# A macaron block with an RWKV mixer: where the second feed-forward layer's modulation chunks are begun

## The chip, the cores and the metric

The kernel runs on one NeuronCore of a Trainium2 chip. The metric is device time in microseconds. A run's time is that of one execution; the kernel before was run three times and profiled once more. Engines are named as the profile names them: PE is TensorE (PEld its weight loads), DVE is VectorE, ACT is ScalarE, POOL is GpSimd and SP is SyncE, which here only issues transfers.

## The reference

One block of 256 tokens with 2048 features. Three sublayers follow one another (a feed-forward layer, a mixer, a second feed-forward layer), each with its own shift, scale and gate out of one modulation vector:

```
mod = (silu(c) @ w_ada + b_ada).reshape(B, 3, 3, D_MODEL)      # w_ada is 2048 x 18432
def swiglu(h, w_gate, w_up, w_down):                            # D_FF = 5632
    return (silu(h @ w_gate) * (h @ w_up)) @ w_down
def sandwich_sublayer(x, fn, gain_pre, gain_post, shift, scale, gate, weight):
    h = rms_norm(x, gain_pre) * (1 + scale) + shift
    y = rms_norm(fn(h), gain_post)
    return x + weight * (1 + gate) * y
x = sandwich_sublayer(x, ffn1,  ..., mod[0, 0], mod[0, 1], mod[0, 2], 0.5)
x = sandwich_sublayer(x, mixer, ..., mod[1, 0], mod[1, 1], mod[1, 2], 1.0)
x = sandwich_sublayer(x, ffn2,  ..., mod[2, 0], mod[2, 1], mod[2, 2], 0.5)
```

All of it is float32. The kernel keeps that precision by splitting each operand into a rounded high part and the remainder (hi and lo) and adding three matmuls.

## The kernel before, in words

**A weight's way.** `load` (L167) has SP issue one transfer into one of four raw buffers. `split` (L173) casts it to hi on ACT (L179), then takes the difference lo on DVE (L180); hi and lo have four buffers each. `mm3` (L186) issues three matmuls per 128 x 128 piece (L189 hi x hT hi, L190 hi x hT lo, L191 lo x hT hi). hT holds the layer's input, transposed, in sixteen feature tiles of 128, each as hi and lo.

**The head of a feed-forward layer.** `outer` (L569) walks over five blocks of features, `FIRST_BLOCKS`: 2, 2, 4, 4 and 4 feature tiles, which the text calls blocks 1 to 5. `q` counts them from 0, and `i` counts ten weight loads in each: two for the first four tiles of the hidden layer (i = 0, 1), eight more (i = 2 to 9) for sixteen further tiles, whose sums are added up in SBUF (L604 a copy on ACT, L606 an addition on DVE). In block 1 those eight are left out and only their `tick` is called; block 2 then loads them for the feature tiles of blocks 1 and 2 at once (the merged loads, 1 MB each). So block 1 has 48 matmuls, block 2 has 48 + 8 x 48, and blocks 3 to 5 have 480 each.

Each block begins with `block(...)`: it finishes the modulation chunk that its features need, updates and scales the residual rows (L517 on DVE, L338 on ACT), transposes them on PE (L353), and makes hT with scale and shift (L357 and L361 on ACT, L362 the difference on DVE).

**A modulation chunk.** The shift and scale (vectors 7 and 6) of one block of features are one chunk, so chunk 3 is that of block 3. `ada_step` (L220) does a quarter of a chunk. For chunks 3, 4 and 5 a step is four tiles of 128 x 1024 in four buffers of their own, each by two transfers of 256 KB on SP (L238), and for each tile one product on DVE: `acc = tile * csilu[k] + acc` (L242 for a chunk's first, L244 for the others). After the fourth step, eight matmuls with a single column (L251, written x8 in the order and x16 in the trace) add up `acc` over partitions, and DVE adds the bias (L264). There is one `acc` buffer. PE, DVE, ACT and SP each work through their own list in order.

**What sets the order.** A scheduler writes the list of each engine before the run, from the program's order and priorities. A step stands in the program where `tick` (called after each load, and for each load left out) or `ada_finish` calls it. In the second layer a step is called at i in `TICKS = (1, 3, 7)` of every block as long as chunk 5 is not done. Chunks 1 and 2 are made in the mixer stage (`ADA_AHEAD = 1`). Three chunks or twelve steps are left: three in each of the blocks 1 to 4. Chunk 3's fourth step so falls into block 2, and chunk 4 ends and chunk 5 begins in block 3.

Of the kernel before, what the change touches and what calls it, by code (L numbers as in the profile page):

```python
# [25 lines left out]
MERGE = 4  # L26
FIRST_BLOCKS = ((0, 2), (2, 2), (4, 4), (8, 4), (12, 4))
TICKS = (1, 3, 7)
GROUPS = (20, 16, 8)
ADA_AHEAD = 1  # L30
ADA_FFN1, ADA_MIXER, ADA_OUT, ADA_FFN2 = 2.8, 3, 3, 12
# [45 lines left out]
class Block:  # L77
# [1124 lines left out]
    def run(self):  # L1202
        I = self.I
        self.constants()
        with ExitStack() as ph:
            mm, actp = self.ffn_pools(ph)
            self.begin(mm)

            def block(k0, n):
                q = [b[0] for b in FIRST_BLOCKS].index(k0)  # L1210
                self.ada_finish(((1, 0), q), mm)
                for tt in range(2):
                    self.pre_rows(tt, k0, n)
                self.pre_block(0, k0, n, mm)

            def tick(q, i):
                if q == len(FIRST_BLOCKS) - 1:
                    if i == 0:
                        self.begin_rest(mm)
                elif i in TICKS:  # L1220
                    self.ada_step(mm)

            self.ffn(I["ffn1_w_gate"], I["ffn1_w_up"], I["ffn1_w_down"], ADA_FFN1, mm, actp, FIRST_BLOCKS, block, tick,
                     FF_OUTER, FF_SPILL, (FF_SPILL + FF_OUTER) // 2 - 8, GROUPS,
                     lambda *a: (self.ada_finish((3,), mm), self.post_begin(0, 0.5, True, mm, *a)), lambda tt: None, True)
        with ExitStack() as ph:
            self.phase(ph, 2, 0, 2, 300)
            self.mixer(ph)
        with ExitStack() as ph:
            mm, actp = self.ffn_pools(ph)  # L1230

            def block(k0, n):
                self.ada_finish(((7, 6), [b[0] for b in FIRST_BLOCKS].index(k0)), mm)
                self.next_block(2, k0, n, mm)

            def tick(q, i):
                if i in TICKS and self.ada_pos < self.ada_end[(7, 6)]:
                    self.ada_step(mm)

            self.ffn(I["ffn2_w_gate"], I["ffn2_w_up"], I["ffn2_w_down"], ADA_FFN2, mm, actp, FIRST_BLOCKS,  # L1240
                     block, tick, FF_OUTER, FF_SPILL, (FF_SPILL + FF_OUTER) // 2 - 8, GROUPS,
                     lambda *a: (self.ada_finish((8,), mm), self.post_begin(2, 0.5, False, mm, *a)),
                     self.store, False)
# [27 lines left out]
```

## Time and profile before

| | before |
|---|---|
| median of three runs | 2172.55 us (2161.99 to 2174.09) |
| the profiled execution's own time | 2168.19 us |
| span of that execution | 2166.3 us |
| mean granted clock of TensorE | 0.986 |
| PE, DVE, ACT busy | 96%, 76%, 50% of the span |
| read from HBM | 497.77 MB |

The span runs from the first to the last instruction; the profiled execution's own time has another 1.9 us around it. The second layer's blocks 1 to 5 lie at 1378 to 1650 us of the span. In a timeline a row has its start, its length (us), engine, line, operation, output and input, count, and in brackets the idle time of that engine before it with what ended it. A row of the windows gives for each engine its busy time and, after an x, its instructions, then the granted clock, the DMA share and GB/s.

### The profile page before, as it was taken

To read this page: it belongs to the slowest core of one execution; us is meant where nothing else is said; L and a number is where in the kernel's file an instruction comes from. 1 tells how busy PE (TensorE), PEld (TensorE's weight loads), DVE (VectorE), ACT (ScalarE), POOL (GpSimd) and SP (SyncE) were. 2 spreads that over 40 slices of the span, in tenths; PEclk is the share of its full clock that TensorE was granted. 3 is DMA by queue.
4 is the path that set the end of the run, shared out by engine and by line. 5 is a ranking of instruction groups with operands and counts; after the bars stand their busy time and mean duration, and the time that the engine had idled before them with its cause. 6 is when DMAs were issued, how large, how long until landed. Compare 5 with 4: busy or idle time off the path is not lost.

```text
span 2166.3 us, 38214 instructions
## 1 busy us (share of the span) xinstructions
PE 2076.9 (96%) x15435; PEld 1828.5 (84%) x15435; DVE 1635.6 (76%) x2543; ACT 1078.5 (50%) x1809; POOL 0.2 (0%) x4
## 2 busy tenths in 40 slices
PE   4999999999999998999999999789999999999998
PEld 3999988888888877888888868689998888888886
DVE  6789897888878778887778776868899655555556
ACT  4534543444433555765656655444454344443453
POOL 0000000000000000000000000000000000000000
PEclk9999999999999999999999999889999999999999
DMA  9999888998888748625332335698888656555553
GB/s 314 359 319 321 282 291 303 330 319 310 310 318 297 270 137 247 195 83 164 103 105 84 99 98 175 233 346 282 305 284 297 237 193 195 186 183 194 195 187 125
DMA packets 313408, 502.40 MB, mean 232 GB/s; under 512 B 12965, under 2 KB 173838, under 8 KB 312974
## 3 DMA queue, kind: packets, MB, share of 16 engines
q1 hardware_dynamic: 311212, 496.32, 68.1%
q10 hardware_dynamic: 2018, 3.62, 0.5%
q8 instruction: 121, 1.98, 0.4%
q14 instruction: 57, 0.47, 0.1%
HBM read 497.77 MB, written 2.12 MB: 231 GB/s over the span
## 4 chain that ended last, share of the span: by engine, by line
PE 79%; DMA 9%; DVE 7%; ACT 3%; issue 2%; SPq 1%; DVEq 0%; ACTq 0%
PE mm L196 15%; PE mm L191 9%; PE mm L190 9%; PE mm L189 9%; PE mm L197 8%; DMA ada<-in_w_ada_dram 6%; PE mm L523 6%; PE mm L524 6%; PE mm L525 6%; DVE lo L180 3%; DVE acc L244 2%; DMA raw<-in_w_in_dram 1%; ACT hi L179 1%; DMA raw<-in_ffn_w_gate_dram 1%; PE mm L251 1%
## 5 line engine op out<-in xcount | busy, mean ns | idle before, releaser
L179 ACT CAST hi<-raw 128x1024 fp32r<-128x1024 f32 (+2 forms) x766 | 694.3, 913 | 798.1 <-PE mm L525 262.8
L180 DVE TENSOR_TENSOR lo<-raw,hi 128x1024 fp32r<-128x1024 f32 (+2 forms) x766 | 797.8, 1051 | 339.7 <-ACT hi L179 336.0
L196 PE MATMUL mm<-hT,hi 128*128 128x512 f32 x1536 | 539.8, 395 | 0.0
L190 PE MATMUL mm<-hT,hi 128*128 128x256 f32 x1824 | 521.6, 287 | 5.4 <-DVE hT L362 5.4
L189 PE MATMUL mm<-hT,hi 128*128 128x256 f32 x1824 | 518.5, 287 | 7.2 <-ACT hT L357 5.6
L191 PE MATMUL mm<-hT,lo 128*128 128x256 f32 x1824 | 522.7, 288 | 1.3 <-DVE lo L180 1.3
L197 PE MATMUL mm<-hT,lo 128*128 128x256 f32 x1536 | 431.8, 281 | 1.6 <-DVE lo L180 1.6
L244 DVE SCALAR_TENSOR_TENSOR acc<-ada,csilu,acc 128x1024 f32<-128x1024 f32 (+1 forms) x300 | 352.5, 1175 | 90.2 <-DMA ada<-in_w_ada_dram 85.7
L189 PEld LDWEIGHTS mm<-hT,hi 128*128 128x128 f32 x1824 | 347.1, 192 | 13.8 <-ACT hT L357 8.3
L190 PEld LDWEIGHTS mm<-hT,hi 128*128 128x128 f32 x1824 | 348.5, 191 | 10.8 <-DVE hT L362 7.5
L191 PEld LDWEIGHTS mm<-hT,lo 128*128 128x128 f32 x1824 | 347.5, 191 | 7.2 <-DVE lo L180 1.9
L196 PEld LDWEIGHTS mm<-hT,hi 128*128 128x128 f32 x1536 | 288.8, 188 | 67.7
L197 PEld LDWEIGHTS mm<-hT,lo 128*128 128x128 f32 x1536 | 288.0, 187 | 2.4 <-DVE lo L180 2.2
L524 PE MATMUL mm<-lo,act 128*128 128x512 f32 (+1 forms) x656 | 252.2, 384 | 0.4 <-DVE lo L180 0.4
L523 PE MATMUL mm<-hi,act 128*128 128x512 f32 (+1 forms) x656 | 252.4, 385 | 0.0
L525 PE MATMUL mm<-hi,act 128*128 128x512 f32 (+1 forms) x656 | 251.9, 384 | 0.0
L524 PEld LDWEIGHTS mm<-lo,act 128*128 128x128 f32 x656 | 123.3, 188 | 25.6 <-DVE lo L180 1.5
L523 PEld LDWEIGHTS mm<-hi,act 128*128 128x128 f32 x656 | 123.3, 188 | 24.5
L525 PEld LDWEIGHTS mm<-hi,act 128*128 128x128 f32 x656 | 123.3, 188 | 24.4
L606 DVE TENSOR_TENSOR act<-act,mm 128x512 f32<-128x512 f32 x96 | 64.2, 682 | 1.9 <-PE mm L191 1.6
L251 PE MATMUL mm<-ones,acc 128*128 128x1 f32 x128 | 18.6, 273 | 34.5 <-DVE acc L244 34.5
L251 PEld LDWEIGHTS mm<-ones,acc 128*128 128x128 f32 x128 | 18.3, 226 | 35.3 <-DVE acc L244 35.2
(371 smaller groups left out, 1965.6 us busy)
## 6 DMA issues: line engine op xcount, KB each, us to landing
raw<-in_ffn_w_down_dram SPq DMA_DIRECT2D x88, 1024.0 KB, 6.2
raw<-in_ffn_w_gate_dram SPq DMA_DIRECT2D x86, 1024.0 KB, 6.9
raw<-in_ffn_w_up_dram SPq DMA_DIRECT2D x86, 1024.0 KB, 5.5
ada<-in_w_ada_dram SPq DMA_DIRECT2D x160, 512.0 KB, 7.0
ada<-in_w_ada_dram SPq DMA_DIRECT2D x256, 256.0 KB, 5.3
raw<-in_w_in_dram SPq DMA_DIRECT2D x34, 1024.0 KB, 6.1
raw<-in_w_out_dram SPq DMA_DIRECT2D x16, 1024.0 KB, 5.3
raw<-in_w_in_dram SPq DMA_DIRECT2D x9, 512.0 KB, 4.6
```

The source lines that it names most:

```text
L179: a = nc.scalar.copy(hi, raw)
L180: d = nc.vector.tensor_tensor(lo, raw, hi.bitcast(F32), ALU.subtract)
L189: nc.tensor.matmul(ps, hi, x[:, 0, :], start=start, stop=False)
L190: nc.tensor.matmul(ps, hi, x[:, 1, :], start=False, stop=False)
L191: nc.tensor.matmul(ps, lo, x[:, 0, :], start=False, stop=stop)
L196: nc.tensor.matmul(ps.rearrange("p a t -> p (a t)"), hi, x.rearrange("p a t -> p (a t)"), start=start, stop=False)
L197: nc.tensor.matmul(ps[:, 0, :], lo, x[:, 0, :], start=False, stop=stop)
L244: self.later(nc.vector.scalar_tensor_tensor(acc, raw[:, i], ck, acc, ALU.mult, ALU.add))
L523: nc.tensor.matmul(ps, x[:, 0, ts], hi, start=start, stop=False)
L524: nc.tensor.matmul(ps, x[:, 0, ts], lo, start=False, stop=False)
L525: nc.tensor.matmul(ps, x[:, 1, ts], hi, start=False, stop=stop)
L606: nc.vector.tensor_tensor(part, part, bank, ALU.add)
```

## The change

In the second feed-forward layer the steps are called at other places: none in block 1, after loads 3, 5, 7 and 9 in block 2, and after loads 1, 3, 5 and 7 in blocks 3 and 4. Each of the chunks 3, 4 and 5 is so begun and ended within one block, the one before the block that needs it. The number of steps, tiles and matmuls is the same.

```
@@ -26,6 +26,7 @@
 FIRST_BLOCKS = ((0, 2), (2, 2), (4, 4), (8, 4), (12, 4))
 TICKS = (1, 3, 7)
+TICKS2 = ((3, 5, 7, 9), (1, 3, 5, 7))
@@ -1234,7 +1235,7 @@
             def tick(q, i):
-                if i in TICKS and self.ada_pos < self.ada_end[(7, 6)]:
+                if q and i in TICKS2[q > 1] and self.ada_pos < self.ada_end[(7, 6)]:
                     self.ada_step(mm)
```

One line is added near the top, so each line number of the changed kernel is one higher than before (L251 becomes L252). The rows below are the lists of three engines.

SP's list at the head of the second layer, before; `raw` are weight tiles (128x2x512 of blocks 1 and 2, 128x4x512 merged), `ada` modulation tiles:

```order
L169 DMA raw_15827<-in_ffn_w_gate_dram 128x2x512
L169 DMA raw_15861<-in_ffn_w_up_dram 128x2x512
L238 DMA ada_15864<-in_w_ada_dram 128x512 x2
L238 DMA ada_15868<-in_w_ada_dram 128x512 x2
L238 DMA ada_15872<-in_w_ada_dram 128x512 x2
L238 DMA ada_15876<-in_w_ada_dram 128x512 x2
L169 DMA raw_15962<-in_ffn_w_gate_dram 128x2x512
L238 DMA ada_15912<-in_w_ada_dram 128x512 x2
L238 DMA ada_15916<-in_w_ada_dram 128x512 x2
L238 DMA ada_15920<-in_w_ada_dram 128x512 x2
L238 DMA ada_15924<-in_w_ada_dram 128x512 x2
L169 DMA raw_15992<-in_ffn_w_up_dram 128x2x512
```

And the same place now:

```order
L170 DMA raw_15827<-in_ffn_w_gate_dram 128x2x512
L170 DMA raw_15861<-in_ffn_w_up_dram 128x2x512
L170 DMA raw_15913<-in_ffn_w_gate_dram 128x2x512
L170 DMA raw_15943<-in_ffn_w_up_dram 128x2x512
L239 DMA ada_16038<-in_w_ada_dram 128x512 x2
L239 DMA ada_16042<-in_w_ada_dram 128x512
L170 DMA raw_15973<-in_ffn_w_gate_dram 128x4x512
L170 DMA raw_16035<-in_ffn_w_up_dram 128x4x512
L239 DMA ada_16042<-in_w_ada_dram 128x512
```

The four weight tiles of blocks 1 and 2 now stand together, and three modulation transfers stand ahead of the first merged load, where 26 stood before. After that SP's list alternates two merged loads with the eight transfers of a step.

PE's list around the reduction of chunk 3, before; `mm` are the banks of sums, `acc` the chunk's products:

```order
L190 MATMUL mm_15804<-hT_94,hi_16021 128x256
L191 MATMUL mm_15804<-hT_94,lo_16022 128x256
L251 MATMUL mm_16010<-ones_71,acc_15863 128x1 x8
L189 MATMUL mm_16051<-hT_94,hi_16053 128x256
L190 MATMUL mm_16051<-hT_94,hi_16053 128x256
```

And now:

```order
L191 MATMUL mm_16397<-hT_94,hi_16426 128x256
L192 MATMUL mm_16397<-hT_94,lo_16427 128x256
L252 MATMUL mm_16474<-ones_71,acc_16037 128x1 x8
L190 MATMUL mm_16485<-hT_94,hi_16487 128x256
L191 MATMUL mm_16485<-hT_94,hi_16487 128x256
```

It stood behind the two small loads of block 2 (row 7721 of the list), ahead of all merged ones; it now stands behind seven of the eight merged loads (row 8057), 48 matmuls before block 3's transposes. In block 3 the reduction of chunk 4 has moved from behind three of the ten loads (row 8252) to behind seven (row 8444), and that of chunk 5 has kept its place in block 4 (row 8927).

DVE's list in block 3 at chunk 4's last products, before; `lo` are splits:

```order
L244 SCALAR_TENSOR_TENSOR acc_16113<-ada_16811,csilu_95,acc_16113 128x1024
L180 TENSOR_TENSOR lo_16772<-raw_16739,hi_16771 128x1024
L244 SCALAR_TENSOR_TENSOR acc_16113<-ada_16815,csilu_95,acc_16113 128x1024
L180 TENSOR_TENSOR lo_16833<-raw_16801,hi_16832 128x1024
L180 TENSOR_TENSOR lo_16861<-raw_16801,hi_16860 128x1024
```

And now:

```order
L245 SCALAR_TENSOR_TENSOR acc_16634<-ada_17055,csilu_95,acc_16634 128x1024
L607 TENSOR_TENSOR act_15809<-act_15809,mm_16989 128x2x256
L245 SCALAR_TENSOR_TENSOR acc_16634<-ada_17059,csilu_95,acc_16634 128x1024
L607 TENSOR_TENSOR act_15810<-act_15810,mm_16990 128x2x256
L245 SCALAR_TENSOR_TENSOR acc_16634<-ada_17063,csilu_95,acc_16634 128x1024
L265 TENSOR_TENSOR mod_105<-mm_17067,cols_29_130 128x4 x2
```

The chunk's last product now stands behind the addition of bank mm_16990, whose last matmul is the row just ahead of the reduction on PE.

On ACT the cast of the first merged load of block 2 (raw_15973) now stands ahead of the four rows that make block 2's hT; before, those four rows came first.

More of the change, by code (lines that the diff above doesn't have):

```diff
@@ L28 @@
 TICKS = (1, 3, 7)
+TICKS2 = ((3, 5, 7, 9), (1, 3, 5, 7))
 GROUPS = (20, 16, 8)
@@ L1236, in tick @@
             def tick(q, i):
-                if i in TICKS and self.ada_pos < self.ada_end[(7, 6)]:
+                if q and i in TICKS2[q > 1] and self.ada_pos < self.ada_end[(7, 6)]:
                     self.ada_step(mm)
```

## The prediction

> **What bounds the kernel now.** The page first:
>
> ```profile
> PE 2076.9 (96%) x15435; PEld 1828.5 (84%) x15435; DVE 1635.6 (76%) x2543; ACT 1078.5 (50%) x1809; POOL 0.2 (0%) x4
> ```
>
> PE is the bound, so its idle or slow stretches are what there is to win. Next the table by windows over the start of the second feed-forward layer (columns: length, then busy us and instruction count of PE, PEld, DVE, ACT and POOL, the granted clock, the DMA share, GB/s):
>
> ```profile
> 1384.00:1388.00 4.00, 2.80 (x22) 2.40 (x21) 4.00 (x6) 2.06 (x3) 0.00 (x0) 1.00 0.71 215
> 1392.00:1396.00 4.00, 4.00 (x19) 3.82 (x19) 3.92 (x5) 0.00 (x0) 0.00 (x0) 0.50 0.92 308
> 1400.00:1404.00 4.00, 0.97 (x9) 0.78 (x7) 4.00 (x6) 1.46 (x3) 0.00 (x0) 0.97 0.72 232
> 1404.00:1408.00 4.00, 0.00 (x0) 0.00 (x0) 3.67 (x4) 1.43 (x2) 0.00 (x0) 0.50 0.94 298
> 1420.00:1424.00 4.00, 4.00 (x21) 4.00 (x20) 3.96 (x5) 0.00 (x0) 0.00 (x0) 0.50 0.99 352
> 1428.00:1432.00 4.00, 4.00 (x37) 4.00 (x36) 2.36 (x2) 2.24 (x4) 0.00 (x0) 1.00 1.05 386
> ```
>
> PE stands still from about 1400 on, and when it works around the hole (1392 to 1396, 1420 to 1424) it does so at clock 0.50 and issues 19 to 21 matmuls where 37 fit. PE's timeline and the list of waits name the culprit:
>
> ```profile
> 1386.47 0.33 PE L353 MATMUL mm<-consts,y 128*128 128x128 f32 x1
> 1388.07 0.55 PE L353 MATMUL mm<-consts,y 128*128 128x128 f32 x3 [1.26 <-ACT y L338]
> 1389.27 0.51 PE L189 MATMUL mm<-hT,hi 128*128 128x256 f32 x2 [0.66 <-ACT hT L357]
> 1391.38 0.58 PE L190 MATMUL mm<-hT,hi 128*128 128x256 f32 x1 [1.61 <-DVE hT L362]
> 1415.85 3.58 PE L251 MATMUL mm<-ones,acc 128*128 128x1 f32 x16 [14.88 <-DVE acc L244]
> 1466.84 1.03 PE L353 MATMUL mm<-consts,y 128*128 128x128 f32 x8
> ...
> 1527.84 1.03 PE L353 MATMUL mm<-consts,y 128*128 128x128 f32 x8
> ```
>
> The L353 rows are the transposes that open blocks 2, 3 and 4. In block 2 PE waits 14.88 us at L251, the reduction of chunk 3, for the last of DVE's sixteen products of that chunk. Nothing needs chunk 3 before 1466.84; PE waits only because L251 stands in its queue ahead of block 2's remaining weights. Behind it, those weights were not much earlier. SP's queue and ACT's cast show it:
>
> ```profile
> 1372.48 0.37 SPq L169 DMA_DIRECT2D raw<-in_ffn_w_gate_dram  x1
> 1372.89 0.46 SPq L169 DMA_DIRECT2D raw<-in_ffn_w_up_dram  x1
> 1373.40 4.70 SPq L238 DMA_DIRECT2D ada<-in_w_ada_dram  x8
> 1378.42 0.38 SPq L169 DMA_DIRECT2D raw<-in_ffn_w_gate_dram  x1
> 1383.71 5.79 SPq L238 DMA_DIRECT2D ada<-in_w_ada_dram  x8
> 1389.54 0.43 SPq L169 DMA_DIRECT2D raw<-in_ffn_w_up_dram  x1
> 1391.02 9.39 SPq L238 DMA_DIRECT2D ada<-in_w_ada_dram  x10
> 1400.51 0.38 SPq L169 DMA_DIRECT2D raw<-in_ffn_w_gate_dram  x1
> ...
> 1408.64 1.99 ACT L179 CAST hi<-raw 128x1024 fp32r<-128x1024 f32 x2 [2.07 <-DMA raw<-in_ffn_w_gate_dram]
> ```
>
> 26 modulation transfers go out ahead of the first merged weight load (1400.51), which lands at 1408.6. With L251 taken away and nothing else, PE would still have stood until about 1410. The change moves both.
>
> **The change part by part.** All times are in the profiled execution.
>
> *Pace of PE.* Two pairs of rows of its timeline, at full and at half clock:
>
> ```profile
> 1470.22 0.28 PE L189 MATMUL mm<-hT,hi 128*128 128x256 f32 x1
> ...
> 1474.11 0.28 PE L191 MATMUL mm<-hT,lo 128*128 128x256 f32 x1
> ...
> 1420.07 0.41 PE L189 MATMUL mm<-hT,hi 128*128 128x256 f32 x1
> ...
> 1423.91 0.41 PE L189 MATMUL mm<-hT,hi 128*128 128x256 f32 x1
> ```
>
> 33 steps in 3.89 us are 0.118 us a matmul; at half clock 18 steps in 3.84 us, 0.213. Block 2 has 48 matmuls for its two small loads and 8 x 48 for the merged ones: 432, or 51.0 us. It takes 1466.84 - 1386.47 = 80.4 us now.
>
> *Block 1, three steps gone.* Twelve modulation tiles leave DVE's and SP's queues there. Block 1's end moves little (its splits gate it): one DVE product of 0.74 us stood between its splits, so the transposes of block 2 come at about 1386.0.
>
> *Start of block 2.* SP now issues four weight loads at once and the fifth, merged one as soon as the first buffer is split. On ACT the cast of that fifth load stands ahead of block 2's hT, so the start hangs on its landing.
>
> ```profile
> 1380.81 0.69 DVE L180 TENSOR_TENSOR lo<-raw,hi 128x512 fp32r<-128x512 f32 x1
> ...
> DMA to landing us min/median/max: 3.7/6.0/8.2
> ```
>
> The buffer is free at 1381.5. From issue to landing weight tiles took 3.7 to 8.2 us, so it lands between 1385.2 and 1389.7. Only the four loads and one and a half modulation tiles stand ahead of it, so I take 4.8, near the low end: 1386.3. ACT's cast (1.05), hT, and on DVE the split of this load and the two hT differences follow; eight matmuls can slip in before. I put steady running at 1390.0 (ends 1389.0 and 1393.0), against 1391.4 at half clock today.
>
> *Rest of block 2.* 424 matmuls at 0.118 are 50.0 us. The reduction of chunk 3 now stands ahead of the last load; at full clock it costs what the chain's row of the next chunk's reduction shows:
>
> ```profile
> 1486.64 1.68 PE mm L251 x16
> ```
>
> 1390.0 + 50.0 + 1.7 = 1441.7, and 1466.84 - 1441.7 is **25.1 us** gained, if PE never waits. What is late next is the chunk's last step. Its products stand in DVE's queue between the splits of the last two loads:
>
> ```profile
> L180 DVE TENSOR_TENSOR lo<-raw,hi 128x1024 fp32r<-128x1024 f32 x82 | 99.5, 1221 | 29.8 <-ACT hi L179 29.6
> L244 DVE SCALAR_TENSOR_TENSOR acc<-ada,csilu,acc 128x1024 f32<-128x1024 f32 x60 | 76.8, 1280 | 4.9 <-DMA ada<-in_w_ada_dram 4.3 <-DVE lo L180 0.4
> L606 DVE TENSOR_TENSOR act<-act,mm 128x512 f32<-128x512 f32 x48 | 32.0, 681 | 0.1
> ```
>
> There are four split buffers, two loads' worth, so the second half of load 10 is cast when PE is done with load 8, after 336 matmuls: 1390.0 + 328 x 0.118 = 1428.7. Cast 1.0, split 1.22 and the last two products at 1.28 make 1433.5. PE reaches the reduction after load 9, at 1390.0 + 376 x 0.118 = 1434.4. That is tight, so I charge a wait of 1 us (0 to 3).
>
> *Block 3.* It now carries four steps instead of three, and DVE's last product of chunk 4 stands behind the addition of the bank that PE finishes just before the reduction. That wait is certain by the order: 0.68 for the addition, 1.28 for the product, some 0.3 of handing over. **2.3 us** lost (2 to 5). In DVE busy time the block needs 20 splits (24.4), 16 additions (10.9), 16 products (20.5) and about 4 for hT and x: 59.8 us in a block of 61.0 today (1466.84 to 1527.84), and consecutive rows overlap a little (1398.30 to 1399.49 is 1.19 for a row of 1.28):
>
> ```profile
> 1398.30 1.28 DVE L244 SCALAR_TENSOR_TENSOR acc<-ada,csilu,acc 128x1024 f32<-128x1024 f32 x1
> 1399.49 0.75 DVE L517 SCALAR_TENSOR_TENSOR x<-y,row,x 128x512 f32<-128x512 f32 x1
> ```
>
> So the fourth step just fits.
>
> *Block 4* also gets a fourth step, but its last product stands 48 matmuls (5.7 us) ahead of its reduction: 0 (0 to 4.8, the step's four products in full). Block 5 has none before and none after.
>
> *Transfers.* By the end of block 2, DMA has 18.9 MB to bring: four loads of 0.5 MB, eight of 1 MB, four steps of 2 MB. Two rows of windows bracket the rate:
>
> ```profile
> 1425.00:1430.00 5.00, 5.00 (x45) 1.00 1.06 395
> ...
> 1470.00:1500.00 30.00, 30.00 (x256) 30.00 (x257) 22.59 (x27) 11.90 (x15) 0.00 (x0) 1.00 0.82 279
> ```
>
> From about 1374.6, at 395 GB/s the last tile lands at 1422.4, at 279 at 1442.3. The second row is of a stretch where buffers, not the engines (share 0.82), held the transfers back, so I take 370: 1425.7, before its product is due. Charge 0.
>
> *Clock.* Before, it fell to 0.50 at 1390 after a stretch (1386.5 to 1391.4) with waits of 1.26, 0.66 and 1.61 us and only six matmuls and transposes. In the stretch that replaces it PE does twelve in about 3.7 us. I take no fall; one costs what it costs here, 6 us at half speed or 3.3 us. [...]
>
> *Sum.* 25.1 - 1.0 - 2.3 = 21.8 us, all on PE's path, since PE is nearly always busy from block 3 to the end. The profiled execution took 2168.19 us (span 2166.3 and 1.9 around it), so 2146.4 by it. It stands 4.4 below the median of the three runs; from the median the same gain gives 2150.8. I write the middle, **2148 us**.
>
> **The rivals.**
> 1. *The clock falls at block 2's start after all.* For it: the row at 0.50. Against: less idleness. Price 3.3, so 2151. Chance 0.15.
> 2. *DVE becomes the bound of blocks 3 and 4.* For it: 59.8 of 61.0 us. Against: an engine in order can be full without PE waiting, since splits run two loads ahead. Four more products in each block, all exposed: 2 x 4 x 1.22 = 9.8 in place of 2.3, so 2155. Chance 0.13.
> 3. *Transfers pace block 2.* At 279 GB/s the last tile lands at 1442.3, its product ends at 1443.6, and the reduction waits 10.2 us instead of 1: 2157. Chance 0.12.
> 4. *Slower: each of the three reductions becomes a wait like the one removed.* Every chunk now ends in the block just before the one that needs it, where chunks 4 and 5 had been begun earlier, so a late last step hits PE three times. The place is L252; at today's 14.88 and 4.0 for the clock behind it (L251's 3.58 against 1.68, and 22 matmuls at 0.213), three waits cost 57 us against the 25 won in block 2: 2168 + 32 = 2200. It decides from a wait of about 8.4 us at each. Against: the order gives 5.7 us of lead in block 4. Chance 0.05.
> 5. *The change does nothing there* is excluded by the order: SP's weight loads and L252 have moved.
>
> **How the numbers follow.** Forecast 0.52, rivals 0.15, 0.13, 0.12 and 0.05, and 0.03 for a gain of under 10 us of another kind. 0.5% of the time is 11 us, about what a measurement of this kernel can tell from no change; it lies at 2158. The forecast and the first rival are faster, and most of the second and third, whose numbers stand near the line: 0.82 faster, 0.13 the same, 0.05 slower. The range: the start at its early end and no waits give 26.3 us, 2143, less 3 for the spread of runs: 2140. Above, it takes in rivals 1 to 3 and 3 us: 2160.
>
> **What would show it.** Right: no wait over 3 us at L252 in block 2, PE at clock 1.00 from 1397 on, block 3's transposes at 1441 to 1445, a wait of 2 to 3 us at L252 in block 3 for acc on DVE, block 4 about as long as today. Wrong: a long wait at L252 for acc with `ada` transfers behind it (rivals 3 and 4), PE waiting for lo in blocks 3 and 4 (rival 2), or block 2's first matmuls at 1393 or later.

## The result, and the profile after

| | before | after |
|---|---|---|
| median of six runs each, taken together | 2169.53 us | 2148.48 us |
| lowest and highest | 2161.99 to 2174.09 | 2142.26 to 2152.82 |
| the profiled execution, its span | 2168.19, 2166.3 | 2142.26, 2140.5 |
| mean granted clock of TensorE | 0.986 | 0.993 |

The changed kernel is faster, by about 1%: the ratio is 0.9904 with a 95% interval of 0.9878 to 0.993, or 21 us with an interval of 15 to 26. The forecast was 2148.

On the page PE's busy time fell by 11 us (2076.9 to 2065.7) and the other engines' hardly; what changed is the time in which PE stood still (span less busy time, 89.4 us before and 74.8 after) or was at half clock (62.5 us and 30.1, from the granted clock in windows of 1 us):

```profile
PE 2065.7 (97%) x15435; PEld 1819.9 (85%) x15435; DVE 1633.9 (76%) x2543; ACT 1078.1 (50%) x1809; POOL 0.2 (0%) x4
```

PE's timeline shows blocks 2 to 4 in ten rows. L354 rows of eight, and the first row, open the blocks; L252 rows are the reductions; a bracket is PE's idle time ahead of the row:

```profile
1379.12 0.60 PE L354 MATMUL mm<-consts,y 128*128 128x128 f32 x4
1380.66 0.39 PE L190 MATMUL mm<-hT,hi 128*128 128x256 f32 x1 [0.95 <-ACT hi L180]
1426.87 1.92 PE L252 MATMUL mm<-ones,acc 128*128 128x1 f32 x16
1434.38 1.04 PE L354 MATMUL mm<-consts,y 128*128 128x128 f32 x8
1436.51 0.74 PE L190 MATMUL mm<-hT,hi 128*128 128x256 f32 x4 [1.09 <-ACT hT L358]
1438.35 0.38 PE L191 MATMUL mm<-hT,hi 128*128 128x256 f32 x1 [1.10 <-DVE hT L363]
1480.37 2.20 PE L252 MATMUL mm<-ones,acc 128*128 128x1 f32 x16 [2.65 <-DVE acc L245]
1500.75 1.04 PE L354 MATMUL mm<-consts,y 128*128 128x128 f32 x8
1543.29 1.84 PE L252 MATMUL mm<-ones,acc 128*128 128x1 f32 x16
1562.04 1.03 PE L354 MATMUL mm<-consts,y 128*128 128x128 f32 x8
```

Block 2 lasts 1434.38 - 1379.12 = 55.3 us against 80.4, and the 14.88 us at its reduction are gone without a wait in their place. Block 3 lasts 66.4 against 61.0; its reduction waits 2.65 us for DVE's last product. Block 4 lasts 61.3 against 59.7. So +25.1, -5.4 and -1.6.

The windows of block 2 (columns as in the prediction) show it without a hole from 1384 to 1424: full clock, 36 matmuls in every 4 us, and a DMA share of over 1, all at once:

```profile
1384.00:1388.00 4.00, 4.00 (x36) 4.00 (x35) 4.00 (x5) 2.40 (x4) 0.00 (x0) 1.00 1.05 387
1400.00:1404.00 4.00, 4.00 (x36) 4.00 (x35) 3.81 (x4) 1.69 (x3) 0.00 (x0) 1.00 1.05 387
1420.00:1424.00 4.00, 4.00 (x36) 4.00 (x36) 3.96 (x4) 1.90 (x3) 0.00 (x0) 1.00 1.03 360
```

Before, the stretches 1400 to 1404 and 1404 to 1408 had 9 and 0 matmuls.

Block 1 begins at 1371.0 in this profile, 7.2 us earlier than in that of before, though PE's list ahead of it is the same. The later profiles show that this moves from run to run (1368.8 to 1381.3 over all kernels of this text), so the lengths of the blocks, not the spans, are compared below.

### The profile page after: what moved, and what is told of

Read it like the earlier page. It is cut to its first block, busy times and chain, and to the rows that moved or that the text cites. A ratio compares the mean times of both kernels' runs of the same rounds, so it can differ in the third digit from the quotient of the medians.

```text
span 2140.5 us, 38232 instructions
## 1 busy us (share of the span) xinstructions
PE 2065.7 (97%) x15435; PEld 1819.9 (85%) x15435; DVE 1633.9 (76%) x2543; ACT 1078.1 (50%) x1809; POOL 0.2 (0%) x4
## 4 chain that ended last, share of the span: by engine, by line
PE 88%; DVE 5%; DMA 3%; ACT 2%; issue 1%; SPq 0%; DVEq 0%; ACTq 0%
PE mm L197 17%; PE mm L192 9%; PE mm L191 9%; PE mm L190 9%; PE mm L198 8%; PE mm L524 8%; PE mm L525 8%; PE mm L526 8%; DVE lo L181 2%; DMA raw<-in_w_in_dram 1%; DVE acc L245 1%; DMA ada<-in_w_ada_dram 1%; PE mm L252 1%; ACT hi L180 1%; PE sb L1111 1%
## 5 line engine op out<-in xcount | busy, mean ns | idle before, releaser
L252 PE MATMUL mm<-ones,acc 128*128 128x1 f32 x128 | 17.3, 263 | 24.1 <-DVE acc L245 24.0
L252 PEld LDWEIGHTS mm<-ones,acc 128*128 128x128 f32 x128 | 17.0, 211 | 25.0 <-DVE acc L245 21.9
```

## The experiments

The theory on trial: block 2's hole had two causes, one behind the other. The reduction of chunk 3 stood too early in PE's list, and modulation transfers stood ahead of weights in SP's. What is left of the cost is block 3's reduction, which DVE's last product reaches late. The rivals: one cause alone would do; only bytes count; block 3's loss is chance.

This is the summary, in us; the sum is that of blocks 1 to 4. Ratios are to the kernel before, measured beside each.

| kernel | block 1 | 2 | 3 | 4 | sum | median and ratio (95%) |
|---|---|---|---|---|---|---|
| before | 8.3 | 80.4 | 61.0 | 59.7 | 209.3 | 2169.53 |
| before, a second profile | 9.6 | 77.6 | 61.0 | 61.1 | 209.3 | |
| after | 8.1 | 55.3 | 66.4 | 61.3 | 191.0 | 2148.48, 0.9904 (0.9878 to 0.993) |
| after, a second profile | 8.1 | 56.9 | 69.4 | 61.3 | 195.7 | |
| after, a third | 8.1 | 55.2 | 67.9 | 61.3 | 192.5 | 2151.54, 0.9926 (0.9901 to 0.9951) |
| steps in block 1, reduction late | 8.3 | 68.7 | 61.1 | 60.9 | 198.9 | 2154.99, 0.9953 (0.9937 to 0.9969) |
| no step in block 1, reduction early | 9.6 | 81.2 | 65.7 | 60.9 | 217.4 | 2170.49, 1.0019 (0.9997 to 1.0041) |
| one step in block 1 | 8.1 | 57.5 | 69.0 | 60.8 | 195.4 | 2148.57, 0.9929 (0.9907 to 0.9952) |
| steps one load sooner | 8.1 | 54.1 | 69.3 | 61.4 | 192.9 | 2151.08, 0.9934 (0.9912 to 0.9956) |
| chunks 3 to 5 left out | 8.1 | 52.7 | 59.4 | 64.1 | 184.3 | one run, 2144.47 |
| reductions two loads later | 8.1 | 55.0 | 60.8 | 61.5 | 185.4 | 2138.87, 0.9887 (0.9864 to 0.991) |
| the same, a second time | 8.1 | 55.1 | 59.0 | 61.5 | 183.7 | 2143.62, 0.9906 (0.9882 to 0.993) |

**The reduction late, the steps still in block 1.** Of each edit only the lines that matter are shown, against the changed kernel. In the edits the table has an entry for each block, and a number that stands more than once calls as many steps.

```diff
-TICKS2 = ((3, 5, 7, 9), (1, 3, 5, 7))
+TICKS2 = ((1, 3, 7), (9,), (1, 3, 5, 7), (1, 3, 5, 7), ())
```

> Three steps stay in block 1 as before; only chunk 3's fourth step moves to the end of block 2, and with it PE's reduction to behind seven merged loads. Blocks 3 and 4 as in the change. SP's list keeps 24 modulation transfers ahead of the first merged weight load. My theory (place of the reduction and place of the weights each cost): PE no longer waits for acc but for the weights that land at about 1408 in the time of the kernel before, so block 2 takes 71 to 74 us (80.4 before, 55.3 changed), the ratio is about 0.999. Rival 1 (the wait at the reduction was all of it): block 2 is 80.4 - 14.9 - 4 = 61.5 us or less. Rival 2 (block 2 is paced by its bytes, 18.9 MB in both): 55 to 58 us, as changed.

Block 2 took 68.7 us, below the 71 to 74 of the theory and far above both rivals. PE's timeline at its head, and SP's rows beside it:

```profile
1380.41 0.55 PE L354 MATMUL mm<-consts,y 128*128 128x128 f32 x3 [1.26 <-ACT y L339]
1383.73 0.58 PE L191 MATMUL mm<-hT,hi 128*128 128x256 f32 x1 [1.61 <-DVE hT L363]
1397.98 0.58 PE L190 MATMUL mm<-hT,hi 128*128 128x256 f32 x1 [4.64 <-ACT hi L180]
...
1440.05 1.84 PE L252 MATMUL mm<-ones,acc 128*128 128x1 f32 x16
```

```profile
1383.36 5.82 SPq L239 DMA_DIRECT2D ada<-in_w_ada_dram  x8
1389.29 0.38 SPq L170 DMA_DIRECT2D raw<-in_ffn_w_gate_dram  x1
```

No reduction waits any more, yet PE comes to the merged weights only at 1397.98, 19 us into the block. Until then it has only the two small loads to work on, from 1384.1 to 1388.6 at about 0.213 us a matmul, the pace of half clock, and then it waits 4.64 us, because the first merged load goes out only at 1389.29, behind 24 modulation transfers. This is the second hole that the prediction saw behind the first.

Block 3 was expected as in the changed kernel (66.4) and took 61.1, and the ratio came out lower than the 0.999 expected. Its four steps and its reduction stand at the same loads, but in DVE's list the chunk's last product now stands well ahead of the last additions. It started 7.6 us before the reduction, which did not wait:

```profile
1482.24 1.28 DVE L245 SCALAR_TENSOR_TENSOR acc<-ada,csilu,acc 128x1024 f32<-128x1024 f32 x1
...
1489.87 1.84 PE L252 MATMUL mm<-ones,acc 128*128 128x1 f32 x16
```

So neither the fourth step nor the reduction's place behind seven loads is enough to make block 3's reduction wait; what decides is the place that the scheduler gives the last product in DVE's list.

**No step in block 1, but the reduction early.** The other half: all four steps are called at load 3 of block 2, and so the reduction stands behind its two small loads and one merged load (one merged load later than before).

```diff
-TICKS2 = ((3, 5, 7, 9), (1, 3, 5, 7))
+TICKS2 = ((), (3, 3, 3, 3), (1, 3, 5, 7), (1, 3, 5, 7), ())
```

> None of chunk 3's steps in block 1, as in the changed kernel, but all four of them, and so its reduction, behind the fourth weight load of block 2 instead of behind the fourth, sixth, eighth and tenth. It is the other half of the pair with the first experiment: there the steps stayed in block 1 and the reduction came late, here no step is in block 1 and the reduction comes early. Theory (what costs is an early reduction in PE's queue, and modulation transfers issued in one bunch ahead of weights): PE reaches the reduction before DVE has its last product, since 8 MB at the 387 GB/s of the changed kernel's block 2 take some 22 us from the bunch's start; a wait of 8 to 12 us at L252 in block 2, a granted clock of 0.50 for some microseconds behind it, block 2 at 66 to 70 us against 55.3. Rival (only the bytes that go ahead of block 2's weights count, and they are gone from block 1): no wait over 2 us, block 2 at 55 to 57. Blocks 3 and 4 as in the changed kernel by both, 66 and 61.

```profile
1414.33 3.55 PE L252 MATMUL mm<-ones,acc 128*128 128x1 f32 x16 [22.89 <-DVE acc L245]
```

The list of waits over block 2 (us in total, times, longest):

```profile
ACT hi L180 <- PE mm L191: 34.9, 15, 21.4
PE mm L252 <- DVE acc L245: 22.9, 1, 22.9
DVE acc L245 <- DMA ada<-in_w_ada_dram: 13.5, 6, 4.3
```

Direction as the theory had it, size twice as large: 22.89 us in place of 8 to 12, and block 2 as long as before. The estimate counted the transfers from the bunch's start. It left out that four modulation buffers let SP go on only as DVE empties them, and that DVE's products took turns with splits and residual rows. The first row excludes the rival: ACT could not cast for 21.4 us at a stretch because PE, which would free the buffers, stood at the reduction. The next two merged loads were split and ready (on DVE the second one's last split ends at 1398.9), 96 matmuls that the reduction kept PE from. The load behind them was issued only at 1401.04, with 23 modulation transfers between the second merged load and it, so the transfers have a part in this hole too. Block 3 took 65.7, near the 66 expected, but not for the reason expected: its reduction did not wait, and 2.29 of the 4.7 us above the kernel before were a wait for hT at its head.

The four kernels make a square. With both causes block 2 has 80.4 us, with the transfers in block 1 alone 68.7, with the early reduction alone 81.2, with neither 55.3. Moving the steps out of block 1 while the reduction stays early gains nothing measurable; doing both gains 25. The corner with the early reduction is not clean: the chunk then has to be made inside block 2, so the reduction waits longer than before (22.89 us against 14.88).

**One step left in block 1.**

```diff
+TICKS2 = ((3,), (5, 7, 9), (1, 3, 5, 7), (1, 3, 5, 7), ())
```

> One step (four tiles, eight transfers) goes back into block 1, between the second and third weight load; three steps in block 2, blocks 3 and 4 as in the change. Theory: 2.1 MB ahead of the third load delay the fifth by 1 to 3 us, nothing else is late: block 2 takes 56 to 59 us against 55.3 changed, no wait over 1 us at its reduction. Rival 2 (bytes pace it): shorter than 55.3, since 2.1 MB come before the block. Rival 3 (any step in block 1 costs a share of the whole): a third of 25 us, 63 us.

Block 2 took 57.5 us, inside the theory's range: one step, eight transfers, ahead of the weights costs 2.3 us against the changed kernel's first profile (0.6 against its second), three steps cost 13.4. Block 3 is like the changed kernel's (69.0), with a wait of 2.21 us at its reduction.

**Steps one load sooner in blocks 3 and 4.**

```diff
+TICKS2 = ((), (3, 5, 7, 9), (0, 2, 4, 6), (0, 2, 4, 6), ())
```

> As the change, but in blocks 3 and 4 the steps stand one load sooner (after loads 0, 2, 4 and 6). PE's reduction of chunk 4 moves with it to behind six loads, and on DVE two products and a split now stand behind the addition of the bank that PE finishes just ahead of the reduction, where one product stood. Theory (the order on DVE makes the wait): the wait at the reduction in block 3 grows from 2.65 to about 4.2 us, block 3 stays at 66 to 68 us; block 4, with its last product ahead of those additions, has no wait. Rival (DVE and the transfers are too full, the last product is late): one load, 5.7 us, more for each step makes no difference to the load, but lets the four steps start sooner, so the wait goes to 0 to 2 us and block 3 falls to 61 to 64 us.

```profile
1480.22 3.54 PE L252 MATMUL mm<-ones,acc 128*128 128x1 f32 x16 [4.78 <-DVE acc L245]
```

As the theory said, steps that are begun sooner help nothing, since the reduction moves with them and DVE's list ahead of it hardly gets shorter: block 3's wait grew from 2.65 to 4.78 us (4.2 were expected), and the block took 69.3, above the 66 to 68 expected.

**The reductions two loads later than their last step.** The step keeps its place; its matmuls and the bias are held back.

```diff
-                if q and i in TICKS2[q > 1] and self.ada_pos < self.ada_end[(7, 6)]:
-                    self.ada_step(mm)
+                for _ in range(TICKS2[q].count(i)):
+                    self.ada_step(mm, True)
+                if i == TICKS2[q][-1] + 2 if TICKS2[q] else False:
+                    self.reduce()
```

> As the change, with the same steps at the same loads, but each reduction is issued two loads after its chunk's last product (in block 2 at the block's end), so no product stands just ahead of it. Theory: no wait at a reduction and no fall of the clock behind it, so block 3 goes from 66.4 to 62 us, block 2 stays at 55 to 57, block 4 at 60 to 61; the ratio to the kernel before is 0.988. Rival (blocks 3 and 4 lose because DVE and the transfers carry a fourth step): block 3 stays at 65 us or more, with PE waiting for splits or hT in place of acc.

PE's row of block 3's reduction and the window around it:

```profile
1487.35 1.84 PE L267 MATMUL mm<-ones,acc 128*128 128x1 f32 x16
```

```profile
1486.00:1488.00 2.00, 2.00 (x20) 2.00 (x19) 1.87 (x3) 0.57 (x1) 0.00 (x0) 1.00 1.05 385
```

No bracket, full clock, block 3 at 60.8 us with its four steps: the 5.4 us that the change lost there are back, and the rival is out. Block 4, at 61.5, was above the 60 to 61 expected.

**The changed kernel and the kernel before once more, and the late reductions beside the changed kernel.** Four further measurements of three kernels, as they are.

> The changed kernel once more, unedited. What is asked is how much of the two profiles' difference is spread from run to run. Theory (block 3's wait and the clock behind it belong to the order of the instructions, the 1.6 us of block 4 and the 7.2 us ahead of the second layer do not): block 2 at 55.0 to 55.5, a wait of 2 to 3.2 us at block 3's reduction, block 3 at 65 to 69, block 4 anywhere from 59.5 to 61.5, the start of block 1 anywhere from 1371 to 1379. Rival (block 3's loss was chance): no wait over 1.5 us there, block 3 at 61 to 62.

> The kernel before once more, unedited, for the same question. Theory: block 2 at 79 to 82 us with a wait of 13 to 16 us at chunk 3's reduction, block 3 at 61, block 4 anywhere from 59.5 to 61.5, the start of block 1 anywhere from 1371 to 1379. Rival (the hole in block 2 varies as much as the gain): block 2 under 77 or over 84.

> The changed kernel, unedited, beside the kernel with the late reductions on one chip, so that the two can be set against each other. Theory (what is left of the change's cost is block 3: a wait of 2.65 us at its reduction, and the stretches of half clock that such a wait sets off, each 3.4 us long and worth some 1.5 us): 2145 to 2153 us, block 3 at 65 to 70 us with a wait of 2.2 to 3.2 at its reduction. Rival (block 3's loss is too small to be seen): no more than 2 us above the other kernel.

> The kernel whose three reductions stand two weight loads behind their chunk's last product, once more, on the same chip as the changed kernel. Theory (no wait at a reduction, so no stretch of half clock in block 3 either): 2137 to 2146 us and 5 to 9 us below the changed kernel; blocks 2, 3 and 4 at 54.5 to 57, 60.5 to 62.5 and 61 to 61.7. Rival (the 10 us between the two earlier measurements were chips and chance): within 2 us of the changed kernel.

The hole of before came back (14.89 us at L251). Its block 2 took 77.6 us, below the 79 to 82 expected, of which block 1 had 1.3 more; block 1 began at 1381.3, later than expected. Block 3's wait in the changed kernel was 2.66 and 2.65 us in the two new profiles: it belongs to the order, not to chance. What changes from run to run is the clock (below); it also took block 2 of the second profile to 56.9, above the 55.5 expected, and block 3 to 69.4, above 69. On one chip the kernel with late reductions had a median 7.9 us lower than the changed one, as expected (5 to 9), but the two intervals overlap, so the times alone do not prove that it is the faster of the two. Block 3 is shorter, at 60.8 and 59.0 against 66.4, 69.4 and 67.9. The 59.0, under the 60.5 expected, has a part that is not the order's: PE ran at the faster of the two paces shown at the end (267 matmuls from 1450 to 1480, where the kernel before had 256 from 1470 to 1500, and 0.113 us a matmul from 1476.9 to 1488.3).

**Chunks 3 to 5 left out.** No step is called in the loop and the vectors are set to zero, so this kernel does not compute the block.

```diff
-                if q and i in TICKS2[q > 1] and self.ada_pos < self.ada_end[(7, 6)]:
-                    self.ada_step(mm)
+                pass
```

> Chunks 3, 4 and 5 of the second layer's modulation are left out (their transfers, DVE's products and the three reductions; the vectors that they give are set to zero), so that blocks 1 to 4 have only their own weights. It is the floor for any placing of these steps. Theory (in the changed kernel block 2 runs at PE's own pace, and block 3 loses only to its reduction): block 2 at 53 to 54 us, against 55.3 with the chunk's 1.7 us of matmuls; block 3 at 59 to 60, block 4 at 59 to 60; no clock under 0.9 from block 2 on. Rival (transfers or DVE hold block 2 or 4 of the changed kernel back): block 2 at 50 or less, or block 4 at 57 or less.

Block 2 took 52.7, just under the 53 expected, and block 3 59.4. It is not quite the floor that it was to be, since the modulation of a later vector moved up into blocks 2 to 4 (11 of its products already in block 2). With 1.9 us for the reduction's own matmuls, block 2 comes to 54.6, an estimate good to a microsecond at best: with the steps one load sooner it took 54.1. The changed kernel's 55.3 leaves about 1 us there. Block 4 was a miss by both theories: 64.1, with 6.8 us of half clock from about 1505 on (0.213 us a matmul behind the second row below), since products of the later vector and splits stood on DVE ahead of hT:

```profile
1502.09 0.74 PE L190 MATMUL mm<-hT,hi 128*128 128x256 f32 x4 [0.61 <-ACT hT L359]
1505.79 0.58 PE L191 MATMUL mm<-hT,hi 128*128 128x256 f32 x1 [2.95 <-DVE hT L364]
```

## Why the prediction was right, and where it was not

**Block 2, 25.1 us: right, term by term.** The fifth load was to land 4.8 us after its issue and PE's start to hang on its cast. SP's row and ACT's row of it:

```profile
1374.34 0.38 SPq L170 DMA_DIRECT2D raw<-in_ffn_w_gate_dram  x1
```

```profile
1379.57 1.04 ACT L180 CAST hi<-raw 128x1024 fp32r<-128x1024 f32 x1 [0.98 <-DMA raw<-in_ffn_w_gate_dram]
```

It landed 5.2 us after issue, and the cast began 0.45 us after block 2's transposes (forecast: 0.3). From the transposes to the reduction were to pass 1434.4 - 1386.0 = 48.4 us and did 47.75. The block from transposes to transposes was to take 55.7 and took 55.3. That the gain is 25.1 to the digit is luck (from the second profile of before, 77.6, it is 20.7 to 22.4); that both holes went is not, as the four kernels show.

**The charge of 1.0 for a wait at block 2's reduction (0 to 3): not needed.** None of the three profiles shows a wait there. The kernel with steps one load sooner, where block 2 is as in the changed one, shows 0.39 us, so the order is as tight as the prediction said.

**Transfers: right, at the upper end.** 370 GB/s were assumed between 279 and 395; the windows of block 2 above show 360 to 387, and in its list of waits DVE waits for no transfer. Rival 3 is out.

**No fall of the clock at block 2's start: right** in all three profiles of the changed kernel (1.00 from 1380 to 1392 in the first, from 1375 to 1391 in the third). With one step left in block 1 it did fall there (0.50 from 1386 to 1388), so it was near.

**Block 3, 2.3 us (2 to 5): the step that was mis-sized.** The mechanism was as told: the reduction waits for the product behind the bank's addition. DVE's rows:

```profile
1476.56 0.68 DVE L607 TENSOR_TENSOR act<-act,mm 128x512 f32<-128x512 f32 x1
1477.15 1.28 DVE L245 SCALAR_TENSOR_TENSOR acc<-ada,csilu,acc 128x1024 f32<-128x1024 f32 x1
1478.35 0.67 DVE L607 TENSOR_TENSOR act<-act,mm 128x512 f32<-128x512 f32 x1
1478.95 1.27 DVE L245 SCALAR_TENSOR_TENSOR acc<-ada,csilu,acc 128x1024 f32<-128x1024 f32 x1
```

PE stopped at 1480.37 - 2.65 = 1477.72. The third product still ran until 1478.35 (0.63, which the prediction did not count), then came the addition (0.60), the last product (1.27) and 0.15 of handing over, where the author's estimate was 0.3: 2.65. So the wait itself lay inside the range of 2 to 5. But the block lost 5.4, because the clock fell behind the wait (0.50 in the windows below). It did so in all five profiles in which block 3's reduction waited (2.21 to 4.78 us), and behind only one of the 24 reductions of chunks 3 to 5 that began without a wait. The windows around it:

```profile
1478.00:1480.00 2.00, 0.00 (x0) 0.00 (x0) 2.00 (x3) 1.70 (x2) 0.00 (x0) 1.00 1.05 397
1480.00:1482.00 2.00, 1.63 (x14) 1.66 (x15) 0.22 (x1) 0.00 (x0) 0.00 (x0) 0.96 1.05 387
1482.00:1484.00 2.00, 2.00 (x10) 2.00 (x11) 1.39 (x4) 0.00 (x0) 0.00 (x0) 0.50 1.05 386
1484.00:1486.00 2.00, 2.00 (x14) 2.00 (x13) 1.18 (x2) 0.00 (x0) 0.00 (x0) 0.68 1.05 387
```

Windows away from a fall show 1.00 and those wholly inside one 0.50. Taken as a mixture of these two, the clock column gives the time at half speed: 2 us x (0.04 + 0.50 + 0.32) / 0.50 = 3.4 us. At 0.213 us a matmul instead of 0.118 that is 16 matmuls instead of 29, a loss of 13 x 0.118 = 1.5 us. The remaining part is at the block's head, where DVE's hT now comes 1.10 us late, behind the splits and products queued ahead of it. The row of before:

```profile
1469.88 0.39 PE L190 MATMUL mm<-hT,hi 128*128 128x256 f32 x1 [0.19 <-DVE hT L362]
```

So 2.65 + 1.5 + 0.9 = 5.1 of 5.4. The other two profiles have the same wait and hT, and more of the clock. The windows of the third:

```profile
1486.00:1488.00 2.00, 1.24 (x11) 1.27 (x12) 0.61 (x1) 0.71 (x1) 0.00 (x0) 0.98 1.05 398
1488.00:1490.00 2.00, 2.00 (x11) 2.00 (x11) 0.69 (x3) 0.00 (x0) 0.00 (x0) 0.50 1.06 389
1490.00:1492.00 2.00, 2.00 (x11) 2.00 (x11) 1.88 (x3) 0.00 (x0) 0.00 (x0) 0.50 1.05 385
1492.00:1494.00 2.00, 2.00 (x12) 2.00 (x11) 0.00 (x0) 0.00 (x0) 0.00 (x0) 0.50 1.09 394
1494.00:1496.00 2.00, 2.00 (x16) 2.00 (x16) 0.50 (x1) 1.05 (x1) 0.00 (x0) 0.82 0.96 316
```

Here it is 2 us x (0.02 + 3 x 0.50 + 0.18) / 0.50 = 6.8 us, two stretches, 3.0 us lost: 2.65 + 3.0 + 0.9 = 6.6 of 6.9. The second profile has three stretches (one of them at the block's head, from 1444 to 1450: 2 us x (0.27 + 0.50 + 0.08) / 0.50 = 3.4) and lost 8.4. So the term was 5.4 to 8.4, not 2.3. Its wait held; what it left out is the half clock behind the wait and the later hT. The prediction asked for the clock at block 2's start, where it did not fall, and not behind the one wait that it called certain.

**Block 4, no loss: right.** No wait at its reduction. The 1.6 us of the first pair of profiles were the other side's: PE ran faster in block 4 of before than in its block 3, at the same clock shown:

```profile
1500.00:1510.00 10.00, 10.00 (x87) 10.00 (x86) 8.72 (x10) 3.85 (x4) 0.00 (x0) 1.00 0.79 245
...
1550.00:1560.00 10.00, 10.00 (x91) 10.00 (x90) 7.02 (x8) 4.05 (x4) 0.00 (x0) 1.00 0.97 356
```

In the second profile of before block 4 took 61.1, against 61.3 in each of the three after. Rival 2 (DVE bounds blocks 3 and 4) is out: with the same four steps and no wait at the reduction block 3 took 61.1 and 60.8. Rival 4 (three long waits) is out too: only block 3's reduction waits, 2.65 us where the rival needed 8.4 at each.

**The sum.** Blocks 1 to 4 shrank from 209.3 to 195.7, 192.5 and 191.0, by 14 to 18 us, where 21.8 were forecast. The first measurement says 21, the second 16 (its ratio of 0.9926). The hit on 2148 therefore owes a few us to luck, to spread outside these blocks: by their lengths the sum was 3.5 to 8.2 us too high. In the first pair of profiles that is 3.1 of block 3 and 1.6 of block 4's pace, less the 1.0 that was not needed.

**Three figures of the working do not come out; none enters the sum.** A fall of 6 us at half speed was priced at 3.3 us. That is what its 28 matmuls take at full clock; what they lose is 28 x (0.213 - 0.118) = 2.7. In rival 3 the product ends at 1443.6 and PE reaches the reduction at 1434.4, so the wait is 9.2, not 10.2. The early end of the range is 25.1 + 1.0 = 26.1, not 26.3.

## What to carry to other kernels

A small matmul that sums up another engine's work belongs in PE's list well behind the last product, not where the program happens to end that product: here the same steps with reductions two loads later gave the lowest times of all (medians of 2138.87 and 2143.62 us, against 2148.48 and 2151.54). Read the other engine's list too: with the same steps at the same loads, the scheduler put block 3's last product right ahead of the reduction in one kernel and 7.6 us ahead of it in another. When one hole is removed, look for the second one directly behind it; here one cure alone gained 9 to 12 us and the other nothing, both together 21 to 25 in block 2. Price a wait of PE with what the clock does behind it: here 2.65 us of waiting cost 4 to 6 (2.65 + 1.5 in the first profile, 2.65 + 3.0 in the third).

## What was not expected of the hardware

**The falls of the clock measured 3.4 us or a multiple of it.** Every fall worked out above is 3.4 us or twice that. At 1390 in the kernel before it was 2 us x (0.47 + 0.50 + 0.50 + 0.24) / 0.50 = 6.8:

```profile
1390.00:1392.00 2.00, 0.61 (x3) 0.62 (x4) 2.00 (x3) 0.59 (x2) 0.00 (x0) 0.53 0.83 269
1392.00:1394.00 2.00, 2.00 (x10) 1.82 (x10) 2.00 (x4) 0.00 (x0) 0.00 (x0) 0.50 0.91 293
1394.00:1396.00 2.00, 2.00 (x11) 2.00 (x11) 1.92 (x3) 0.00 (x0) 0.00 (x0) 0.50 0.93 323
1396.00:1398.00 2.00, 1.44 (x8) 0.94 (x6) 0.84 (x1) 1.67 (x2) 0.00 (x0) 0.76 1.05 397
```

Over the whole spans of the first profiles of before and after, in windows of 1 us, the falls measure 3.4, 6.8, 10.2 and, at the reduction of before, 20.5 us, but for the one in which each span ends (4.5 and 6.2). With one order, block 3 of the changed kernel lost one stretch of 3.4 us in the first profile, two in the third and three in the second. What fixes the length is not shown.

The waits behind which it fell differ: at 1390 the clock fell behind three waits in 4.9 us, none over 1.61 us, and it fell behind the waits of 2.65, 2.66 and 2.65 us in three profiles of three. Behind the latter come the sixteen narrow matmuls of the reduction, about 2 us, so the share of the wait alone is not known there; but with the chunks left out the clock also fell behind a wait of 2.95 us for hT (0.213 us a matmul behind it), with no reduction near.

**It fell once behind a reduction that did not wait.** In the second profile of the changed kernel the reduction of block 2 began without a wait at 1431.41 and took 1.92 us, sixteen matmuls of one column, and soon after it:

```profile
1434.00:1436.00 2.00, 2.00 (x15) 2.00 (x14) 2.00 (x2) 0.00 (x0) 0.00 (x0) 0.67 0.91 326
1436.00:1438.00 2.00, 2.00 (x11) 2.00 (x11) 0.00 (x0) 0.73 (x1) 0.00 (x0) 0.50 1.01 382
1438.00:1440.00 2.00, 2.00 (x19) 2.00 (x19) 1.65 (x2) 0.91 (x2) 0.00 (x0) 0.98 1.04 393
```

PE was busy throughout (2.00 of 2.00 us in each of these windows) and the clock fell all the same for 3.4 us; block 2 took 56.9 instead of 55.3, the 1.5 us of one stretch. Whether the narrow matmuls have a part in it is not shown: no run varied their width, and behind the 23 other reductions that began without a wait the clock did not fall.

**Two paces at one clock.** 87 or 91 matmuls per 10 us (0.118 or 0.113 us a matmul) at a granted clock of 1.00 (rows of block 3 and 4 of before, above). What sets them stays open; no experiment was made on it.
